# The sample's delta rule as two pairs of heads on 128 partitions instead of four heads on 64

## The chip, the cores and the metric

The kernel runs on one NeuronCore of a Trainium2 chip. The metric is device time in microseconds (us) of one execution. The engines named below are PE (TensorE matmul), DVE (VectorE), ACT (ScalarE), POOL (GpSimd) and SP (which issues most DMAs). PE works on fp32 data here in two ways: the large projections use fp32r operands split into a high and a low part, the small matrices of the delta rule use plain fp32, for which the trace shows two passes per product (and one pass per transpose).

## The reference, cut to what matters

One layer of a hybrid encoder is computed for two request groups that share weights: a prompt of 512 tokens and a sample of 64 tokens. The layer has a mixer (a gated delta rule with 4 heads of 128 x 128 state, and a differential attention with 4 heads), a cross attention to 256 memory tokens, and a feed-forward block of width 4096. The part that changes is the gated delta rule, in chunks of tokens:

```python
diff = G[..., :, None] - G[..., None, :]               # G: running sum of the gates
gam  = where(tril, exp(where(tril, diff, 0)), 0)
kk   = einsum('nbhid,nbhjd->nbhij', kc, kc)
a_sys = where(strict, bc[..., :, None] * kk * gam, 0) + eye(C)
u = triangular_solve(a_sys, bc[..., None] * vc)
w = triangular_solve(a_sys, (bc * exp(G))[..., None] * kc)
qk = einsum('nbhid,nbhjd->nbhij', qc, kc) * gam
...
vn = u - w @ S
o  = qg @ S + qk @ vn
S  = S * gl + kd.T @ vn                                # per head, chunk after chunk
```

The prompt starts from a zero state, the sample from `state_gdn`. The output `o` is normalised per head and token, and gated by silu(z).

## The kernel before, in words

All activations lie transposed, features on partitions and 576 tokens (512 prompt, then 64 sample) in the free dimension. The kernel runs through these stages: norm and transposes of x; twelve projections with a short convolution that give q, k and v of the delta rule (lines 401 to 419, kept in `cT`, a tile of [128, 4 heads, 576] for each); the gates (lines 430 to 496); the delta rule (lines 544 to 746); differential attention with its own projections (lines 776 to 893); memory keys and values, output projection, cross attention and the feed-forward block. A projection (`project`, line 165) is a run of matmuls into a bank tagged `pr`: 512 columns per pass with the high weights `wh`, 256 with the low weights `wl`, or 320 columns for the second part of the tokens.

The delta rule goes over five chunks (line 545): chunks 0 to 3 are 128 tokens of the prompt each, chunk 4 is the 64 tokens of the sample. For each chunk `gdn_prep` (line 566) does what doesn't need the state. For n tokens it transposes k, q and v of each head to tokens on partitions, makes the decay matrix `gam` (gates broadcast through a matmul with `triu`, exp on ACT, mask on POOL, line 603), KK times gam as `At`, KQ times gam, and then inverts the triangular matrix by doubling blocks (lines 632 to 680): at each level a masked part `B` of `At`, a product B,Dt that ACT copies to `Y`, a product with `X` that DVE subtracts from `Dt`, and transposes of `Dt` that ACT copies to `X`. With n = 64 that is one starting transpose and levels 2, 4, 8, 16, 32; with n = 128 level 64 comes on top. Every one of these steps loops over 4 heads, so that for chunk 4 each is four matmuls on 64 x 64 of the array.

`gdn_scan` (line 683) then goes through the state of a chunk: k times S, X times r, the output (q times S plus KQ times vn, two matmuls per head into one bank), kd times vn, the state's update on DVE, the norm, transposes, and the gate. Chunk 4 loads its own state S. At the top (lines 731 to 742) `gdn_prep` of chunk c + 1 is called ahead of `gdn_scan` of chunk c.

What stands where on each engine is decided when the program is built, by a scheduler that interleaves independent work, with program order as the priority: projections of z and of the differential attention are put between the steps of the delta rule. On its engine every instruction then runs in that order, and waits for its operands. PSUM banks are few: `pr` has three, `ba` two, and `g0`, `g1` (even and odd chunks) and `gs` (the scan) one each.

Of the kernel before, what the change touches and what calls it, by code (L numbers as in the profile page):

```python
# [8 lines left out]
F32 = mybir.dt.float32  # L9
F32R = mybir.dt.float32r  # L10
AF = mybir.ActivationFunctionType
# [23 lines left out]
def hybrid_layer_kernel(  # L35
# [107 lines left out]
    G.affine_select(out=triu, in_=triu, pattern=[[1, P]], compare_op=ALU.is_ge, fill=0.0, base=0, channel_multiplier=-1)  # L143

# [256 lines left out]
    for typ in (1, 0, 2):  # L401
        cT[typ] = (e5[:, 1], e2[:, 1], e2[:, 0])[typ]
        for h in range(H):
# [12 lines left out]
            A.activation(cT[typ][:, h, :SEQ], yv[:, :SEQ], AF.Silu)  # L416
            A.activation(cT[typ][:, h, SEQ:], yv[:, SOFF:n], AF.Silu)
# [18 lines left out]
    abT = small("p0", [16, T])  # L436
# [9 lines left out]
    for t, (t0, n) in enumerate(TT):  # L446
        tr(b[:n, t * 16 : t * 16 + 16], abT[:, t0 : t0 + n])
    ab2 = const([P, 5, 16], "ab2")
    V.memset(ab2[DEC:, 4, :], 0.0)
    V.tensor_copy(ab2[:, :4, :], b[:, :64].rearrange("p (t c) -> p t c", c=16))  # L450
    V.tensor_copy(ab2[:DEC, 4, :], b[:DEC, 64:80])
# [30 lines left out]
    V.tensor_scalar(gg, t3, -1.0, None, ALU.mult)  # L482
    V.memset(gg[DEC:, 4, :], 0.0)
# [12 lines left out]
    A.activation(kdc, kdc, AF.Exp)  # L496

# [46 lines left out]
    ck, cq, cv_ = cT[1], cT[0], cT[2]  # L544
    chunks = [(c, c * 128, c * 128, 128) for c in range(4)] + [(4, 512, 512, 64)]

    def v4(ap, n):
        return ap.rearrange("p (h n) -> p h n", h=4)[:, :, :n]
# [17 lines left out]
    def gdn_prep(c, c0, n):  # L566
        L = slice(c0, c0 + n)

        def st(tag):
            return sb(dict(gam="Y", sq="B", eg="B").get(tag, tag) + str(c % 2))  # L570

        r8 = tiny([P, 8], "tg")
        s8 = tiny([P, 8], "tg")
        bk = bank(f"g{c % 2}")
        for h in range(H):
            tr(bk[:n, h * P : (h + 1) * P], ck[:, h, L])
        kd = sb("kd")
        V.tensor_tensor(kd[:n], v4(bk, P)[:n], kdc[:n, c, :].unsqueeze(2).to_broadcast([n, 4, P]), ALU.mult)
        sq = st("sq")
        A.activation(sq[:n], v4(bk, P)[:n], AF.Square)  # L580
        V.tensor_reduce(s8[:n, 0:4], sq[:n], AX.X, ALU.add)
        bq = bank(f"g{c % 2}")
        for h in range(H):
            tr(bq[:n, h * P : (h + 1) * P], cq[:, h, L])
        sq2 = st("sq")
        A.activation(sq2[:n], v4(bq, P)[:n], AF.Square)
        V.tensor_reduce(s8[:n, 4:8], sq2[:n], AX.X, ALU.add)
        V.tensor_scalar(s8[:n], s8[:n], EPS, None, ALU.add)
        rpow(r8[:n], s8[:n])
        brk = tiny([P, 4], "tg")  # L590
        V.reciprocal(brk[:n], s8[:n, 0:4])
        V.tensor_tensor(brk[:n], brk[:n], beta[:n, c, :], ALU.mult)

        bg = bank(f"g{c % 2}")
        for h in range(H):
            mm(bg[:, h * P : h * P + n], bc(gg[:n, c, h : h + 1], [n, P]), triu[:n, :n])
        gam = st("gam")
        for h in range(H):
            V.tensor_scalar(
                gam[:n, h, :n], bg[:n, h * P : h * P + n], Gc[:n, c, h : h + 1], 0.0, ALU.subtract, ALU.min  # L600
            )
        A.activation(gam[:n, :, :n], gam[:n, :, :n], AF.Exp)
        G.tensor_tensor(gam[:n, :, :n], gam[:n, :, :n], triu[:n, :n].unsqueeze(1).to_broadcast([n, 4, n]), ALU.mult)
        bkk = bank(f"g{c % 2}")
        for h in range(H):
            mm(bkk[:n, h * P : h * P + n], ck[:, h, L], ck[:, h, L])
        At = st("At")
        for h in range(H):
            V.scalar_tensor_tensor(
                At[:n, h, :n], bkk[:n, h * P : h * P + n], brk[:n, h : h + 1], gam[:n, h, :n], ALU.mult, ALU.mult  # L610
            )
        bkq = bank(f"g{c % 2}")
        for h in range(H):
            mm(bkq[:n, h * P : h * P + n], ck[:, h, L], cq[:, h, L])
        KQ = sb("KQ")
        V.tensor_tensor(KQ[:n, :, :n], v4(bkq, n)[:n], gam[:n, :, :n], ALU.mult)
        nk, rq2 = tiny([P, 4], "tg"), tiny([P, 4], "tg")
        V.tensor_tensor(nk[:n], s8[:n, 0:4], r8[:n, 0:4], ALU.mult)
        V.tensor_scalar(r8[:n, 4:8], r8[:n, 4:8], P ** -0.5, None, ALU.mult)
        V.tensor_tensor(rq2[:n], r8[:n, 4:8], r8[:n, 4:8], ALU.mult)  # L620
        bv = bank(f"g{c % 2}")
        for h in range(H):
            tr(bv[:n, h * P : (h + 1) * P], cv_[:, h, L])
        vb = sb("vb")
        V.tensor_tensor(vb[:n], v4(bv, P)[:n], nk[:n].unsqueeze(2).to_broadcast([n, 4, P]), ALU.mult)
        if c > 0:
            eg = st("eg")
            A.activation(eg[:, :, :n], v4(bg, n), AF.Exp)
            G.tensor_tensor(ck[:, :, L], ck[:, :, L], eg[:, :, :n], ALU.mult)
            G.tensor_tensor(cq[:, :, L], cq[:, :, L], eg[:, :, :n], ALU.mult)  # L630

        def masked(lv):
            B = st("B")
            V.scalar_tensor_tensor(  # L634
                B[:n, :, :n], lev[:n, :n].unsqueeze(1).to_broadcast([n, 4, n]), float(lv), At[:n, :, :n],
                ALU.is_equal, ALU.mult,
            )
            return B

        X = sb("X")  # L640
        Dt = st("Dt")
        B = masked(1)
        V.tensor_tensor(X[:n, :, :n], ident[:n, :n].unsqueeze(1).to_broadcast([n, 4, n]), B[:n, :, :n], ALU.subtract)
        bt = bank(f"g{c % 2}")
        for h in range(H):
            tr(bt[:n, h * P : h * P + n], X[:n, h, :n])
        A.copy(Dt[:n, :, :n], v4(bt, n)[:n])
        lv = 2
        while lv < n:
            Y = st("Y")  # L650
            by = bank(f"g{c % 2}")
            if lv < 64:
                B = masked(lv)
                for h in range(H):
                    mm(by[:n, h * P : h * P + n], B[:n, h, :n], Dt[:n, h, :n])
                A.copy(Y[:n, :, :n], v4(by, n)[:n])
                bx = bank(f"g{c % 2}")
                if 2 * lv < n:
                    for h in range(H):
                        mm(bx[:n, h * P : h * P + n], X[:n, h, :n], Y[:n, h, :n])  # L660
                    V.tensor_tensor(Dt[:n, :, :n], Dt[:n, :, :n], v4(bx, n)[:n], ALU.subtract)  # L661
                    bt = bank(f"g{c % 2}")
                    for h in range(H):
                        tr(bt[:n, h * P : h * P + n], Dt[:n, h, :n])
                    A.copy(X[:n, :, :n], v4(bt, n)[:n])  # L665
                else:
                    for h in range(H):
                        mm(bx[:n, h * P : h * P + n], Y[:n, h, :n], X[:n, h, :n])
                    V.tensor_tensor(X[:n, :, :n], X[:n, :, :n], v4(bx, n)[:n], ALU.subtract)
            else:  # L670
                for h in range(H):
                    mm(by[64:, h * 64 : h * 64 + 64], At[:64, h, 64:], Dt[:64, h, :64])
# [8 lines left out]
        return dict(kd=kd, vb=vb, X=X, KQ=KQ, brk=brk, rq=r8[:, 4:8], rq2=rq2)  # L681

    def gdn_scan(c, c0, t0, n, q, S):
        L = slice(c0, c0 + n)
        if S is None:
            r = q["vb"]
        else:
            b = bank("gs")
            for h in range(H):
                mm(b[:n, h * P : (h + 1) * P], ck[:, h, L], S[:, h, :])  # L690
            r = sb("r", 1)
            V.tensor_tensor(r[:n], q["vb"][:n], v4(b, P)[:n], ALU.subtract)
        b = bank("gs")
        for h in range(H):
            mm(b[:n, h * P : (h + 1) * P], q["X"][:n, h, :n], r[:n, h, :])
        vn = sb("vn", 1)
        V.tensor_tensor(vn[:n], v4(b, P)[:n], q["brk"][:n].unsqueeze(2).to_broadcast([n, 4, P]), ALU.mult)
        bo = bank("gs")
        for h in range(H):
            o = bo[:n, h * P : (h + 1) * P]  # L700
            if S is not None:
                mm(o, cq[:, h, L], S[:, h, :], stop=False)
            mm(o, q["KQ"][:n, h, :n], vn[:n, h, :], start=S is None)
        b = bank("gs")
        for h in range(H):
            mm(b[:, h * P : (h + 1) * P], q["kd"][:n, h, :], vn[:n, h, :])
        Sn = S
        if S is None:
            Sn = sb("S")
            A.copy(Sn, v4(b, P))  # L710
# [487 lines left out]
```

## Time and profile before

| what | value |
|---|---|
| time, three runs | 1060.57, 1061.35 and 1063.02 us, median 1061.35 |
| the profiled execution's own time | 1062.43 us |
| its span, first to last instruction | 1060.4 us, granted PE clock 0.996 |
| busy: PE / PE weight loads / DVE / ACT / POOL | 1037.9 / 931.6 / 671.3 / 432.4 / 72.8 us |
| matmuls | 6574 |
| DMA | 89.96 MB, mean 85 GB/s |

The execution that was profiled took 2.0 us more than its span, and 1.1 us more than the median. In the rows below a line is: start in us, length in us, engine, source line, operation, written tile <- read tiles, shapes (for PE first the part of the array that is used, rows*columns, then the streamed operand), and xN where N neighbours were merged; in brackets stands idle time of the engine ahead of it and what ended it. Matmuls overlap in time, so the cost of one on PE is read from its start to the next one's start.

### The profile page before, as it was taken

What the parts mean: (1) busy time and instruction counts of PE and PEld (TensorE: products, weight loads), DVE (VectorE), ACT (ScalarE), POOL (GpSimd) and SP (SyncE); (2) the same over time, 40 slices, a digit from 0 to 9 for tenths busy, and PEclk for the clock granted to TensorE, in tenths of its full rate; (3) what the DMA queues carried; (4) which work ended last, traced back from release to release, by engine and by line L of the source; (5) the groups of instructions that cost most, each with busy time, mean ns of one, the idle gap of its engine ahead of it and who ended that gap; (6) DMA issues with size and microseconds to landing.
All of it is one profiled execution on the core that took longest, in us unless ns stands there. A gap on an engine that the chain in (4) does not pass through costs nothing.

```text
span 1060.4 us, 16925 instructions
## 1 busy us (share of the span) xinstructions
PE 1037.9 (98%) x6574; PEld 931.6 (88%) x6574; DVE 671.3 (63%) x1471; ACT 432.4 (41%) x897; POOL 72.8 (7%) x126
## 2 busy tenths in 40 slices
PE   8999999999999999999999999999999999999997
PEld 6999889898788877999887799999999999999986
DVE  6766684766466675564554666666666666666764
ACT  6644754333256665443333443323232323222344
POOL 4311120221000000000000000000000000000000
PEclk9999999999999999999999999999999999999999
DMA  7342310100132255634211222132414141323312
GB/s 212 109 126 70 122 40 21 43 1 22 41 100 64 69 187 193 176 87 139 58 42 40 59 81 63 58 100 60 117 49 123 42 119 50 110 60 110 90 50 90
DMA packets 139442, 89.96 MB, mean 85 GB/s; under 512 B 5522, under 2 KB 130576, under 8 KB 138852
## 3 DMA queue, kind: packets, MB, share of 16 engines
q1 hardware_dynamic: 138996, 88.24, 28.0%
q8 instruction: 52, 0.85, 0.3%
q10 hardware_dynamic: 368, 0.66, 0.2%
q14 instruction: 26, 0.21, 0.1%
HBM read 79.14 MB, written 9.74 MB: 84 GB/s over the span
## 4 chain that ended last, share of the span: by engine, by line
PE 88%; issue 4%; DVE 3%; ACT 2%; POOL 1%; DMA 1%; POOLq 0%; ACTq 0%; DVEq 0%
PE pr L103 68%; PE g L103 9%; PE gs L103 5%; PE ba L109 2%; PE g L109 2%; DMA raw<-in_w_ff_dram 1%; POOL tg L204 1%; PE ba L103 1%; DVE B L634 0%; ACT wh L157 0%; DVE wl L158 0%; POOL tiny L204 0%; PE pr L109 0%; DVE Dt L661 0%; PE gs L109 0%
## 5 line engine op out<-in xcount | busy, mean ns | idle before, releaser
L103 PE MATMUL pr<-u,wh 128*128 128x512 f32 (+1 forms) x2664 | 699.5, 344 | 1.2 <-DVE u L288 0.5
L103 PEld LDWEIGHTS pr<-u,wh 128*128 128x128 f32 x2664 | 457.7, 189 | 37.7 <-issue 1.5
L103 PE MATMUL pr<-u,wl 128*128 128x256 f32 (+1 forms) x1776 | 486.8, 300 | 0.0
L103 PEld LDWEIGHTS pr<-u,wl 128*128 128x128 f32 x1776 | 329.2, 189 | 8.3 <-issue 1.0
L157 ACT CAST wh<-raw 128x1024 fp32r<-128x1024 f32 (+1 forms) x153 | 136.5, 892 | 235.0 <-PE pr L103 223.2
L158 DVE TENSOR_TENSOR wl<-raw,wh 128x1024 fp32r<-128x1024 f32 (+1 forms) x153 | 157.4, 1029 | 60.4 <-ACT wh L157 58.5
L944 DVE TENSOR_TENSOR u<-u,pr 128x256 f32<-128x256 f32 (+1 forms) x160 | 72.4, 453 | 62.8 <-PE pr L103 60.2
L204 POOL TENSOR_TENSOR tiny<-tiny,nhalf 128x1 f32<-128x1 f32 (+4 forms) x11 | 10.1, 915 | 663.6 <-DVE tiny L1128 409.7
L197 ACT CAST u<-p 128x256 fp32r<-128x256 f32 x64 | 27.8, 434 | 51.8 <-DVE p L1065 51.8
L103 PE MATMUL pr<-wh,u 128*128 128x512 f32 x128 | 42.3, 404 | 0.0
L198 DVE TENSOR_TENSOR u<-p,u 128x256 fp32r<-128x256 f32 x64 | 29.3, 457 | 15.1 <-ACT u L197 15.1
L190 ACT COPY p<-pr 128x256 f32<-128x256 f32 (+1 forms) x44 | 16.4, 373 | 51.8 <-PE pr L103 51.8
L191 DVE TENSOR_TENSOR p<-pr,p 128x256 f32<-128x256 f32 (+1 forms) x44 | 18.6, 423 | 26.8 <-ACT p L190 26.8
L946 DVE TENSOR_TENSOR u<-u,pr 128x256 f32<-128x256 f32 x80 | 33.6, 420 | 2.4
L1064 DVE TENSOR_TENSOR p<-pr,rB 128x320 f32<-128x320 f32 x32 | 15.7, 492 | 25.7 <-PE pr L103 25.7
L415 DVE SCALAR_TENSOR_TENSOR p<-p,gcol,p 128x579 f32<-128x579 f32 x33 | 27.1, 821 | 6.4 <-ACT p L413 5.9
L1065 DVE SCALAR_TENSOR_TENSOR p<-p 128x256 f32<-128x256 f32 x64 | 29.3, 458 | 2.2
L665 ACT COPY X<-g 128x512 f32<-128x512 f32 (+1 forms) x24 | 13.2, 549 | 42.6 <-PE g L109 42.5
L200 ACT ACTIVATE u<-u,gcol 128x256 fp32r<-128x256 f32 (+1 forms) x32 | 17.0, 534 | 31.1 <-DVE u L946 31.1
L103 PE MATMUL g<-u,qz 128*128 128x256 f32 (+4 forms) x96 | 29.6, 412 | 0.0
L103 PEld LDWEIGHTS pr<-wh,u 128*128 128x128 f32 x128 | 23.6, 188 | 4.7 <-issue 0.2
L634 DVE SCALAR_TENSOR_TENSOR B<-lev,At 128x512 f32<-128x512 f32 (+1 forms) x30 | 20.8, 698 | 10.6 <-PE g L103 8.8
(315 smaller groups left out, 1214.3 us busy)
## 6 DMA issues: line engine op xcount, KB each, us to landing
raw<-in_w_ff_dram SPq DMA_DIRECT2D x32, 512.0 KB
raw<-in_w_ff_dram SPq DMA_DIRECT2D x64, 256.0 KB
raw<-in_w_in_dram SPq DMA_DIRECT2D x28, 512.0 KB
raw<-in_w_mem_k_dram SPq DMA_DIRECT2D x8, 512.0 KB
raw<-in_w_mem_v_dram SPq DMA_DIRECT2D x8, 512.0 KB
raw<-in_w_out_dram SPq DMA_DIRECT2D x8, 512.0 KB
raw<-in_w_mem_q_dram SPq DMA_DIRECT2D x8, 512.0 KB
raw<-in_w_mem_o_dram SPq DMA_DIRECT2D x8, 512.0 KB
```

The lines of the kernel that those rows point to most:

```text
L103: i = nc.tensor.matmul(out, lhsT, rhs, start=start, stop=stop)
L109: i = nc.tensor.transpose(out, in_, ident[:n, :n])
L157: A.copy(wh, raw)
L158: V.tensor_tensor(wl, raw, wh.bitcast(F32), ALU.subtract)
L197: A.copy(h, src)
L198: V.tensor_tensor(lo, src, h.bitcast(F32), ALU.subtract)
L204: G.tensor_tensor(out, in_, bc(nhalf[: in_.shape[0], 0:1], list(in_.shape)), ALU.pow)
L415: V.scalar_tensor_tensor(yv[:, :n], cb[:, i : i + n], cwt[:, m, i : i + 1], yv[:, :n], ALU.mult, ALU.add)
L634: V.scalar_tensor_tensor(B[:n, :, :n], lev[:n, :n].unsqueeze(1).to_broadcast([n, 4, n]), float(lv), At[:n, :, :n], ALU.is_equal, ALU.mult,)
L944: V.tensor_tensor(hm, hm, b, ALU.add)
L946: V.tensor_tensor(hm, hm, more, ALU.add)
L1065: V.scalar_tensor_tensor(f, f, 0.0, f, ALU.max, ALU.mult)
```

## The change

The sample's delta rule (chunk 4) is regrouped: two heads' tokens lie under each other on 128 partitions. What was four heads with 64 x 64 matrices becomes two pairs with 128 x 128 matrices that are block diagonal; the masks `triu2` and `ones2` (two blocks of 64) keep the heads of a pair apart, and the inversion stops at level 32 as before. In `cT` the sample's tokens are kept apart from the prompt's, so that two heads' 64 tokens are 128 neighbouring columns. The per-token columns (gates, their running sums, beta, decay) get copies in the pairs' layout, with a second running sum through `triu2` and `ones2`. In the scan of the sample the states of a pair stand beside each other as 256 columns, and `vn` is laid out as [128, pair, head, 128] with zeros where token and head don't belong together. The prompt's chunks keep their steps; they are written through the same helpers. The core of the diff:

```diff
+    ones2, triu2 = const([P, P], "ones2"), const([P, P], "triu2")
+    G.memset(ones2, 0.0)
+    for i in range(2):
+        R = slice(i * DEC, (i + 1) * DEC)
+        G.memset(ones2[R, R], 1.0)
+    G.tensor_tensor(triu2, triu, ones2, ALU.mult)
...
-        cT[typ] = (e5[:, 1], e2[:, 1], e2[:, 0])[typ]
+        flat = (e5[:, 1], e2[:, 1], e2[:, 0])[typ].rearrange("p k t -> p (k t)")
+
+        cT[typ] = [ap.rearrange("p (h t) -> p h t", h=H) for ap in (flat[:, : H * SEQ], flat[:, H * SEQ :])]
...
+    V.tensor_copy(abT[:, T:], abT[:, SEQ:T])
...
+    def halves_of(dst, src):
+
+        for i in range(2):
+            R = slice(i * DEC, (i + 1) * DEC)
+            V.tensor_copy(dst[R], src[R, 4, i::2])
+
+    halves_of(gg2, gg)
     V.memset(gg[DEC:, 4, :], 0.0)
...
+    halves_of(beta2, beta)
...
+    gsum2 = bank()
+    mm(gsum2[:, 0:2], triu2, gg2)
+    mm(gsum2[:, 2:4], ones2, gg2)
+    V.tensor_copy(Gc2, gsum2[:, 0:2])
+    V.tensor_tensor(kdc2, gsum2[:, 2:4], Gc2, ALU.subtract)
+    A.activation(kdc2, kdc2, AF.Exp)
...
+    chunks = [(c, 4, slice(c * P, (c + 1) * P)) for c in range(4)] + [(4, 2, slice(SEQ, T))]
...
+        def each(f, *args):
+
+            b = bank(f"g{c % 2}")
+            for i in range(nb):
+                f(b[:, i * P : (i + 1) * P], *(x(i) for x in args))
+            return v4(b, nb)
...
-        bkk = bank(f"g{c % 2}")
-        for h in range(H):
-            mm(bkk[:n, h * P : h * P + n], ck[:, h, L], ck[:, h, L])
+        bkk = each(mm, kb, kb)
...
+    def gdn_scan_sample(q, S):
...
+        b = pairs(each(lambda o, i: mm(o, kb(i), S2[:, i, :])))
...
+        def out(o, i):
+            mm(o, qb(i), S2[:, i, :], stop=False)
+            mm(o, q["KQ"][:, i, :], vw[:, i, :], start=False)
+
+        bo = pairs(each(out))
+        S = next_state(c, S, v4(each(lambda o, i: mm(o, q["kd"][:, i, :], vw[:, i, :])), 4))
+        on = sb("on", 1)[:, :nb]
+        normed(q, nb, [(R, bo[R, :, i, :]) for i, R in enumerate(own)], on)
...
+    A.copy(oa[:, 0, :, SEQ:], cT[0][1])
+    V.tensor_tensor(oa[:, 1, :, SEQ:], cT[0][1], oa[:, 0, :, SEQ:].bitcast(F32), ALU.subtract)
```

Since the scheduler sees other instructions, it also sets other orders. First, PE in the inversion of chunk 4, one level of it, before (`Dt` and `B` of this chunk, `pr` a projection, `on` and `gs` the scan of chunk 3):

```order
L109 MATMUL g_456_2561<-ident,Dt_439_2494 64x64 x4
L103 MATMUL pr_3122<-u_94,wh_3097 128x320
L103 MATMUL pr_3122<-u_94,wl_3098 128x320 x2
L103 MATMUL pr_3122<-u_94,wh_3097 128x320
L103 MATMUL g_458_2568<-Dt_439_2494,B_459_2569 64x64 x4
L109 MATMUL gs_2645<-ident,on_2637 128x128 x4
L103 MATMUL g_460_2576<-Y_457_2567,X_2493 64x64 x4
```

The same place now:

```order
L109 MATMUL g_457_2546<-ident,Dt_440_2497 128x128 x2
L103 MATMUL gs_2599<-vn_2588,kd_2202 128x128
L103 MATMUL pr_3091<-u_100,wl_3067 128x320
L103 MATMUL pr_3091<-u_100,wh_3066 128x320
L103 MATMUL g_460_2553<-Dt_440_2497,B_459_2551 128x128 x2
L103 MATMUL pr_3091<-u_100,wh_3066 128x320
L103 MATMUL pr_3124<-u_99,wh_3120 128x512
L103 MATMUL pr_3124<-u_99,wl_3121 128x256
L103 MATMUL g_461_2557<-Y_458_2550,X_2496 128x128 x2
```

Each group of four on 64 columns is now a group of two on 128 columns, and projections are spread otherwise between them.

Second, POOL at the start of the delta rule, before (`tg` is the power that gives 1/norm of a chunk, line 204; `Y` is `gam` of chunk 0, then of chunk 1, line 603):

```order
L204 TENSOR_TENSOR tg_1292<-tg_1293,nhalf 128x8
L204 TENSOR_TENSOR tg_1487<-tg_1488,nhalf 128x8
L603 TENSOR_TENSOR Y_176_1322<-Y_176_1322,triu 128x512
L603 TENSOR_TENSOR Y_226_1517<-Y_226_1517,triu 128x512
L204 TENSOR_TENSOR tiny_1203<-tiny_1201,nhalf 128x1
```

And now (the same lines have become 211 and 644):

```order
L211 TENSOR_TENSOR tg_1311<-tg_1312,nhalf 128x8
L644 TENSOR_TENSOR Y_177_1341<-Y_177_1341,triu 128x512
L211 TENSOR_TENSOR tg_1506<-tg_1507,nhalf 128x8
L644 TENSOR_TENSOR Y_227_1536<-Y_227_1536,triu 128x512
L211 TENSOR_TENSOR tiny_1222<-tiny_1220,nhalf 128x1
```

The mask of chunk 0 moved ahead of the power of chunk 1.

On ACT, a silu of z (line 562 before, 594 now) moved ahead of the table load and the exp that the chain of the gates needs (line 469 before, 477 now), and the exp of `kdc` (496, now 514) moved ahead of such a silu.

More of the change, by code (lines that the diff above doesn't have):

```diff
@@ L541, in hybrid_layer_kernel, with blocks, v4 @@
         V.tensor_tensor(lev, lev, triu, ALU.mult)
[L544 to L548, printed above, removed]
+    chunks = [(c, 4, slice(c * P, (c + 1) * P)) for c in range(4)] + [(4, 2, slice(SEQ, T))]
+    def blocks(typ, c, L):
+        if c < 4:
+            ap = cT[typ][0][:, :, L]
+        else:
+            ap = cT[typ][1].rearrange("p h t -> p (h t)").rearrange("p (b n) -> p b n", b=2)
+        return ap, lambda i: ap[:, i, :]
+    def v4(ap, nb):
+        return ap.rearrange("p (h n) -> p h n", h=4)[:, :nb, :]
     def sb(tag, bufs=2):
@@ L638, in masked @@
             return B
-        X = sb("X")
+        X = sb("X")[:, :nb]
         Dt = st("Dt")
         B = masked(1)
[L643 to L647, printed above, removed]
+        V.tensor_tensor(X, over(ident), B, ALU.subtract)
+        A.copy(Dt, each(tr, of(X)))
         lv = 2
-        while lv < n:
+        while lv < size:
@@ L680, in gdn_prep, with next_state, normed, gdn_scan @@
             lv *= 2
-        return dict(kd=kd, vb=vb, X=X, KQ=KQ, brk=brk, rq=r8[:, 4:8], rq2=rq2)
-    def gdn_scan(c, c0, t0, n, q, S):
-        L = slice(c0, c0 + n)
+        return dict(kd=kd, vb=vb, X=X, KQ=KQ, brk=brk, rq=rq, rq2=rq2)
+    def next_state(c, S, b):
+        if S is None:
+            S = sb("S")
+            A.copy(S, b)
+        else:
+            for h in range(H):
+                V.scalar_tensor_tensor(S[:, h, :], S[:, h, :], egl[:, c, h : h + 1], b[:, h, :], ALU.mult, ALU.add)
+        return S
+    def normed(q, nb, parts, out):
+        so, co = tiny([P, nb], "tg"), tiny([P, nb], "tg")
+        for R, src in parts:
+            A.activation(out[R], src, AF.Square)
+        V.tensor_reduce(so, out, AX.X, ALU.add)
+        V.tensor_tensor(so, so, q["rq2"], ALU.mult)
+        V.tensor_scalar(so, so, 1.0 / P, EPS, ALU.mult, ALU.add)
+        rpow(co, so)
+        V.tensor_tensor(co, co, q["rq"], ALU.mult)
+        for R, src in parts:
+            V.tensor_tensor(out[R], src, co[R].unsqueeze(2).to_broadcast(list(src.shape)), ALU.mult)
+    def gdn_scan(c, L, q, S):
+        (_, kb), (cq, qb) = (blocks(typ, c, L) for typ in (1, 0))
+        wide = [P, 4, P]
+        def each(f):
+            b = bank("gs")
+            for h in range(H):
+                f(b[:, h * P : (h + 1) * P], h)
+            return v4(b, 4)
         if S is None:
@@ L698, in gdn_scan @@
[L698 to L710, printed above, removed]
-        else:
-            for h in range(H):
-                V.scalar_tensor_tensor(
-                    Sn[:, h, :], S[:, h, :], egl[:, c, h : h + 1], b[:, h * P : (h + 1) * P], ALU.mult, ALU.add
-                )
@@ L725, in gdn_scan @@
-        bt = bank("gs")
-        for h in range(H):
-            tr(bt[:, h * P : h * P + n], on[:n, h, :])
-        V.scalar_tensor_tensor(cq[:, :, L], v4(bt, n), gn, zs[:, :, t0 : t0 + n], ALU.mult, ALU.mult)
-        return Sn
+            b = each(lambda o, h: mm(o, kb(h), S[:, h, :]))
+            r = sb("r", 1)
+            V.tensor_tensor(r, q["vb"], b, ALU.subtract)
+        b = each(lambda o, h: mm(o, q["X"][:, h, :], r[:, h, :]))
+        vn = sb("vn", 1)
+        V.tensor_tensor(vn, b, q["brk"].unsqueeze(2).to_broadcast(wide), ALU.mult)
@@ new lines, in out @@
+        def out(o, h):
+            if S is not None:
+                mm(o, qb(h), S[:, h, :], stop=False)
+            mm(o, q["KQ"][:, h, :], vn[:, h, :], start=S is None)
+        bo = each(out)
+        b = each(lambda o, h: mm(o, q["kd"][:, h, :], vn[:, h, :]))
+        S = next_state(c, S, b)
+        on = sb("on", 1)
+        normed(q, 4, [(slice(0, P), bo)], on)
+        bt = each(lambda o, h: tr(o, on[:, h, :]))
+        V.scalar_tensor_tensor(cq, bt, gn, zs[:, :, L], ALU.mult, ALU.mult)
```

201 lines of the change are left out of this document (96 added, 105 removed).

## The prediction

> **What bounds the kernel now.** I read the page first (busy time, then the chain that ended last), then PE's timeline in the stretch of the sample's chunk, then the timelines of PE, POOL and ACT where the delta rule begins. The page:
>
> ```profile
> PE 1037.9 (98%) x6574; PEld 931.6 (88%) x6574; DVE 671.3 (63%) x1471; ACT 432.4 (41%) x897; POOL 72.8 (7%) x126
> PE 88%; issue 4%; DVE 3%; ACT 2%; POOL 1%; DMA 1%; POOLq 0%; ACTq 0%; DVEq 0%
> ```
>
> PE is busy for 98% of the span and is 88% of the chain that ended last; while the delta rule goes through its steps, projections fill PE. So the change is worth what it takes off PE's own row, plus idle time of PE that comes or goes. What it does to DVE and ACT counts only where PE waits. Busy time hides cost, though, since matmuls overlap; I go by starts. Two groups of chunk 4 among projections (four transposes, then a product of four heads, two passes each):
>
> ```profile
> 274.13 0.41 PE L109 MATMUL g<-ident,Dt 64*64 64x64 f32 x4
> 274.47 0.39 PE L103 MATMUL pr<-u,wl 128*128 128x256 f32 x1
> 274.69 0.40 PE L103 MATMUL pr<-u,wh 128*128 128x512 f32 x1
> 274.93 0.28 PE L103 MATMUL pr<-u,wl 128*128 128x256 f32 x1
> 275.04 0.40 PE L103 MATMUL pr<-u,wh 128*128 128x512 f32 x1
> 275.37 0.67 PE L103 MATMUL g<-Dt,B 64*64 64x64 f32 x8
> 275.98 0.39 PE L103 MATMUL pr<-u,wl 128*128 128x256 f32 x1
> 276.20 0.40 PE L103 MATMUL pr<-u,wh 128*128 128x512 f32 x1
> 276.44 0.28 PE L103 MATMUL pr<-u,wl 128*128 128x256 f32 x1
> 276.55 0.39 PE L103 MATMUL pr<-u,wh 128*128 128x512 f32 x1
> ```
>
> An undisturbed 512 pass takes 276.44 - 276.20 = 0.24 us to the next start, a 256 pass 276.55 - 276.44 = 0.11. The 512 pass ahead of the product takes 0.33 (0.09 too much), the 256 pass behind it 0.22 (0.11 too much), the product itself 0.61. So one such group costs PE 0.81, and the transposes cost 0.34 + 0.11 behind + 0.09 ahead (taken alike) = 0.54. Now the same kinds of step on the full array, from chunks 1 and 2:
>
> ```profile
> 189.84 0.60 PE L109 MATMUL g<-ident,u 128*128 128x128 f32 x4
> 190.20 0.36 PE L103 MATMUL pr<-u,wl 128*128 128x256 f32 x1
> 190.40 0.39 PE L103 MATMUL pr<-u,wh 128*128 128x512 f32 x1
> ...
> 191.17 0.46 PE L103 MATMUL gs<-S,u 128*128 128x128 f32 x2
> ...
> 193.03 1.06 PE L103 MATMUL g<-u 128*128 128x128 f32 x8
> ```
>
> Four transposes and the 256 pass behind them take 0.56, that is 0.11 for each transpose and no edge. Sixteen passes of 128 columns take 193.03 - 191.17 = 1.86, 0.116 each, and nothing is lost between the two kinds in them (S, then KQ). So the full array pays by streamed columns alone, and the quarter array pays 0.2 us per group at its edges, and more inside.
>
> **Part by part: PE in chunk 4.** Columns streamed hardly change in the inversion (eight passes of 64 become four of 128); the edges go. Twelve products (two in each of five levels, KK and KQ): 0.81 becomes 4 x 0.116 = 0.46, 0.35 each, **-4.2**. Five groups of transposes (one at the start, four in the levels): 0.54 becomes 2 x 0.11 = 0.22, **-1.6**. The transposes of k, q and v: 12 become 6 at 0.11, **-0.7**. The gates' broadcast: eight passes become four, **-0.5** at 0.116. Then the scan, its first, second and third product before:
>
> ```profile
> 278.13 1.09 PE L103 MATMUL gs<-S,u 128*64 128x128 f32 x8
> ...
> 280.23 1.08 PE L103 MATMUL gs<-on,X 64*64 64x128 f32 x8
> ...
> 282.32 0.43 PE L103 MATMUL gs<-S,u 128*64 128x128 f32 x2
> ...
> 285.20 0.56 PE L103 MATMUL pr<-u,wh 128*128 128x320 f32 x2
> ```
>
> k times S is about 1.0 and two edges of 0.1, and becomes four passes of 256 columns, 0.93 at twice 0.116: -0.3. X times r, 1.2 with its edges, becomes four of 128: -0.7. The output took 285.20 - 282.32 = 2.88 for sixteen passes, 1.0 more than the sixteen above, since it alternates between two parts of the array; it becomes eight of 256, 1.86: -1.2 with its outer edges. kd times vn and the last transposes: -0.5. Scan **-2.7**. Together -9.7.
>
> Against that stands waiting. A group that finds its operand late shows it so, here on the full array:
>
> ```profile
> 155.02 0.36 PE L103 MATMUL pr<-u,wl 128*128 128x256 f32 x1
> 155.43 1.16 PE L103 MATMUL g<-Y,X 128*128 128x128 f32 x8
> 156.43 0.28 PE L103 MATMUL g<-Dt,B 128*128 128x128 f32 x1
> ```
>
> The 256 pass ahead lasts 0.41 instead of 0.11, the group 1.00 instead of 0.93: 0.37. The steps of chunk 4 are one chain, and the copies between them don't get shorter (ACT and DVE move 256 elements per partition as before), while PE's part does. I take five of some 27 groups to wait so, **+1.9**; bounds 0 and all 27, +10. I take a value near the low end because projections still stand between nearly all steps in the new order. The second running sum (`gsum2`) is four passes: **+0.5**. The extra DVE and POOL instructions (copies of columns, two masks, zeros in `vn`) lie on engines that PE doesn't wait for, except at the gates, next. If that cover failed, each would cost about its own length, 0.06 to 0.2 us.
>
> **Part by part: the start of the delta rule.** Here the order moved, and PE was idle:
>
> ```profile
> 107.91 1.28 ACT L469 ACT_TABLE_LOAD   x1
> 109.20 0.22 ACT L469 ACTIVATE t<-t 128x20 f32<-128x20 f32 x1
> 115.88 0.37 PE L103 MATMUL ba<-gg,triu 128*128 128x20 f32 x2 [0.60 <-DVE gg L483]
> 128.96 1.64 POOL L204 TENSOR_TENSOR tg<-tg,nhalf 128x8 f32<-128x8 f32 x1 [2.08 <-DVE tg L588]
> 130.57 1.28 POOL L603 TENSOR_TENSOR Y<-Y,triu 128x512 f32<-128x512 f32 x1
> 133.06 1.23 PE L103 MATMUL g<-u,u 128*128 128x128 f32 x8 [2.07 <-DVE At L609]
> 133.97 0.74 PE L103 MATMUL pr<-u,wh 128*128 128x512 f32 x1
> ...
> 137.08 0.56 PE L103 MATMUL g<-u 128*128 128x128 f32 x2
> ```
>
> At the gates a silu now stands ahead of the exp, so the exp starts about 1.0 us later (an add on DVE, then the silu, ahead of the same 1.28 us load), and with it the long DVE chain to `gg`; two small copies come on top, 0.3. PE has five more projection passes of 320 columns ahead of that product (0.15 each, from 0.24 for 512). So the idle 0.60 becomes about 0.6 + 1.3 - 0.7 = 1.2: **+0.6**.
>
> Then KQ of chunk 0 waits 2.07 us for `At`, which needs the mask on POOL; and that mask stood in POOL's queue behind the power of chunk 1, 128.96 to 130.57. In the new order it stands ahead of it. So it starts with its own operand (the exp on ACT, which by my count of the ACT rows ends at about the same time as before, near 128.1) instead of at 130.57: up to 2.4 earlier. PE also arrives about half a microsecond sooner. Idle 2.07 becomes 0.3: **-1.8**. And behind that idle time PE ran at half clock, by the windows:
>
> ```profile
> 134.00:137.00 3.00, 3.00 (x11) 2.60 (x11) 1.98 (x4) 2.97 (x4) 2.64 (x2) 0.50 0.25 58
> ```
>
> From 133.97 to 137.08 stand five 512 and four 256 passes, which take 1.64 at 0.24 and 0.11: 1.5 lost, **-1.5**. [...]
>
> Last, by the new order of PE the projections run up to 3.5 us ahead in the first three heads of the differential attention, which leaves less cover for its waits there: **+0.5**, bounds 0 and 3.5.
>
> **The sum**, against the profiled span: 1060.4 - 9.7 + 1.9 + 0.5 + 0.6 - 1.8 - 1.5 + 0.5 = 1050.9, 9.5 less. The profiled execution took 1062.43, the median is 1061.35; 9.5 off the median gives 1051.9.
>
> **The rivals.**
>
> A. The edges are waits for operands, not the price of changing the part of the array in use; then they stay. Of the -9.7, 0.2 us at each of some 22 edges is 4.4, and the time returns to 1056.3. For it: the groups' operands do come from ACT and DVE just ahead. Against it: the output of the scan pays 1.0 us for alternating although all its operands are there. Chance 0.10, 1055 to 1058.
>
> B. The start gains nothing, or loses: PE's wait for `At` stays, or the later `gg` leaves PE idle for 2 us, and half clock follows as at 134. Then -3.3 falls away and up to 1.5 comes: 1055.2 to 1056.7. [...] That rule alone has 0.02, B in all 0.17.
>
> C. Slower: the attention's heads run dry. The projections that move ahead are missing in heads 0 to 2, and PE waits in their softmax chains. It would take 0.5 us in each of the 20 tiles to eat the whole gain, 10 us, and more to give 1062 to 1066; it decides from 0.5 us per tile. Against it: in this stretch PE's row has no idle time before, and 3.5 us over the fifteen tiles of heads 0 to 2 is 0.2. Chance 0.05.
>
> ```profile
> 300.00:400.00 100.00, 99.99 (x588) 82.06 (x588) 68.34 (x224) 62.02 (x204) 4.17 (x6) 1.00 0.32 102
> ```
>
> D. More is gained: PE waits in chunk 4 no more than the projections cover (0 instead of 1.9), and idle time elsewhere in the prompt's chunks, whose order moved too, shrinks by a microsecond or two. 1047 to 1049.5. Chance 0.10.
>
> **How the numbers follow.** The forecast (0.58) has 1049.5 to 1055 as its own range. The range over the cases, 1047.5 to 1058, leaves out C, and the edges of A and D. A measurement of this kernel can tell 0.2%, 2.1 us, so faster means under 1059.2: nearly all of the forecast, A, B and D, 0.90; within 0.2% takes A's and B's upper tail, 0.05; slower is C, 0.05.
>
> **What would show it.** In the profile after: PE's rows of chunk 4 in the form 128*128 x4 with 256 passes behind them at 0.2 or less, and the output of the scan at about 1.9 us; PE's product of `gg` at an idle of 1 to 1.5 and KQ of chunk 0 at under 0.8, with 1.00 as granted clock behind it; the start of the state's update of chunk 4 (PE, kd times vn) still with idle time near 0.8 to 1.0, since the norm's chain through POOL stays. I am wrong if PE's passes around chunk 4 keep edges of 0.1, if new idle times above 1 us stand in PE's waits between 140 and 420 us, or if the granted clock shows a second stretch of 0.50.

## The result and the profile after

The changed kernel took 1054.21 us (median of four runs, 1053.19 to 1054.83), the kernel before 1060.96 beside it (1060.31 to 1063.02). The ratio is 0.9936, 95% interval 0.9924 to 0.9947: 6.75 us less, where 9.5 were forecast. The profiled execution took 1053.76 with a span of 1052.0.

Busy time and the chain that ended last, on the page after:

```profile
PE 1027.7 (98%) x6488; PEld 925.7 (88%) x6488; DVE 673.8 (64%) x1478; ACT 433.7 (41%) x900; POOL 73.1 (7%) x130
PE 88%; DVE 5%; issue 3%; ACT 2%; POOL 1%; DMA 1%; POOLq 0%; ACTq 0%; SPq 0%; DVEq 0%
```

PE is still busy for 98%, with 86 passes fewer; the share of DVE in the chain grew from 3 to 5%. PE's timeline in chunk 4, one of the new groups that waits for its operand and one that hardly does, and the weight load of the first, which names the wait:

```profile
262.19 0.45 PE L103 MATMUL pr<-u,wh 128*128 128x320 f32 x2
262.58 0.71 PE L103 MATMUL g<-Dt,B 128*128 128x128 f32 x4
263.05 0.39 PE L103 MATMUL pr<-u,wl 128*128 128x320 f32 x1
...
270.09 0.68 PE L103 MATMUL g<-Dt,B 128*128 128x128 f32 x4
270.53 0.36 PE L103 MATMUL pr<-u,wl 128*128 128x256 f32 x1
270.73 0.39 PE L103 MATMUL pr<-u,wh 128*128 128x512 f32 x1
```

```profile
262.58 0.52 PEld L103 LDWEIGHTS g<-Dt,B 128*128 128x128 f32 x4 [0.20 <-ACT X L685]
```

The product at 270.09 costs 0.44 and 0.08 at the pass behind it (0.20 instead of 0.117): 0.52. The one at 262.58 costs 0.47, 0.08 behind it, and 0.10 ahead, where two passes of 320 take 0.39 instead of 0.29 until it starts: 0.65. Counted so, the twelve products of chunk 4 take 6.8 us, 0.57 each, against 0.81 for the group before that the prediction showed and the forecast's 0.46. In all ten products of the levels the first weight load starts 0.05 us after the copy on ACT that releases it; in the kernel before, one of the ten came so close.

PE's timeline at the start of the delta rule, the waits in it (dots between):

```profile
116.41 0.37 PE L103 MATMUL ba<-gg,triu 128*128 128x20 f32 x2 [0.72 <-DVE gg L500]
...
130.74 1.16 PE L103 MATMUL g<-u,u 128*128 128x128 f32 x8 [0.26 <-DVE At L648]
131.65 0.36 PE L103 MATMUL pr<-u,wl 128*128 128x256 f32 x1
131.86 0.40 PE L103 MATMUL pr<-u,wh 128*128 128x512 f32 x1
132.10 0.28 PE L103 MATMUL pr<-u,wl 128*128 128x256 f32 x1
...
137.77 1.10 PE L109 MATMUL ba<-ident,u 128*128 128x128 f32 x8 [0.81 <-DVE tiny L234]
...
151.50 0.33 PE L109 MATMUL g<-ident,Dt 128*128 128x128 f32 x1 [1.03 <-DVE Dt L684]
```

The idle time of 2.07 ahead of KQ is 0.26, and a 512 pass behind it takes 0.24 where such passes took 0.43 before, with 1.00 as granted clock from 131 to 137 us, so the half clock is gone. But two idle times are new: 0.81 for the transposes of the memory tokens, 1.03 for a `Dt` of chunk 0.

Where the time went, by stretches of PE's row. From the length of each stretch I take what its passes cost undisturbed (0.235 us for 512 columns of a projection, 0.147 for 320, 0.117 for 256, 0.87 ns per column for all others, from the 0.112 at which passes of 128 columns follow each other); waits, edges and low clock are left. "Before" is a second profiled execution of the kernel before (span 1058.6; its run stands with the experiments), since in the first the passes ran slowly for longer at the start. Chunk 4 starts on PE just ahead of the sixth row, which also holds the last part of chunk 3.

```
stretch of PE                           before   after   change
start to 30 us                            8.06    8.06     0.0
30 us to the product of gg                2.28    2.95    +0.7
gg to KQ of chunk 0                       3.10    1.89    -1.2
KQ of chunk 0 to idle at vb (200 us)      8.26    9.48    +1.2
to kd times vn of chunk 2                 4.34    4.46    +0.1
to the last transposes of chunk 4        11.43    5.57    -5.9
to the norm of attention head 0           6.69    5.81    -0.9
the rest                                 13.54   13.51     0.0
passes themselves, undisturbed          990.55  989.44    -1.1
```

That is 7.1 less up to the last matmul, and 6.6 in the spans. The row of chunk 4 gave 5.9, and chunk 4 most of the 1.1, about as much as the whole. The start of the delta rule (rows two to four), forecast at -2.7, lost 0.7; 0.45 of that is the second running sum `gsum2`, which stands there and was forecast apart at +0.5.

### The profile page after: what moved, and what is told of

Same layout as the page of the kernel before. It is cut to its first block, busy times and chain, and to the rows that moved or that the text cites. A ratio compares the mean times of both kernels' runs of the same rounds, so it can differ in the third digit from the quotient of the medians.

```text
span 1052.0 us, 16768 instructions
## 1 busy us (share of the span) xinstructions
PE 1027.7 (98%) x6488; PEld 925.7 (88%) x6488; DVE 673.8 (64%) x1478; ACT 433.7 (41%) x900; POOL 73.1 (7%) x130
## 4 chain that ended last, share of the span: by engine, by line
PE 88%; DVE 5%; issue 3%; ACT 2%; POOL 1%; DMA 1%; POOLq 0%; ACTq 0%; SPq 0%; DVEq 0%
PE pr L103 69%; PE g L103 9%; PE gs L103 5%; PE ba L109 2%; PE g L109 2%; DMA u<-in_cache_mem_k_dram 1%; DVE wl L165 1%; POOL tg L211 1%; PE ba L103 0%; DMA S<-in_state_gdn_dram 0%; POOL tiny L211 0%; DVE B L668 0%; DVE X L674 0%; DVE Dt L684 0%; PE pr L109 0%
## 5 line engine op out<-in xcount | busy, mean ns | idle before, releaser
L164 ACT CAST wh<-raw 128x1024 fp32r<-128x1024 f32 (+1 forms) x153 | 136.4, 892 | 233.7 <-PE pr L103 220.1
```

What stands on the lines that cost most here:

```text
L164: A.copy(wh, raw)
```

## The experiments

The times stand against the kernel before on the same chip, 1060.3 to 1060.7 us.

**a1: only the order on POOL.** The kernel before, with one dependency more, without a semaphore:

```diff
         rpow(r8[:n], s8[:n])
+        if c == 1:
+            tc.add_manual_dep(
+                nc.cur_bb.bb.instructions[-1], mask0[0],
+                mybir.DependencyInfo(mybir.DependencyClass.NoSync, mybir.DependencyReason.DATA),
+                reason="mask first",
+            )
...
+        if c == 0:
+            mask0.append(nc.cur_bb.bb.instructions[-1].name)
```

> The kernel before, with one order changed: on POOL the mask of chunk 0 stands ahead of the power of chunk 1, as in the changed kernel. Chunk 4 stays in four heads. By the prediction's step for the start of the delta rule (idle ahead of KQ 2.07 to 0.3, half clock behind it gone) it is 3.3 us faster than before, near 1057.7 us. Rival, read from the trace of the changed kernel (two new idle times of 0.81 and 1.03 us at 137.8 and 151.5): the chain of chunk 0 runs on DVE and ACT, PE only reaches its next wait sooner, and 0 to 1 us is left, 1060 to 1061; then the idle of 2.07 is gone in the profile and new ones of 1 to 2 us in all stand between 135 and 155 us.

Measured: 1059.07 us, ratio 0.9985 (0.9977 to 0.9994), 1.6 less. Its PE at the same place:

```profile
129.99 0.49 PE L103 MATMUL g<-u 128*128 128x128 f32 x2 [0.45 <-ACT B L638]
130.31 1.06 PE L103 MATMUL g<-u,u 128*128 128x128 f32 x8
...
134.06 0.66 PE L109 MATMUL g<-ident,u 128*128 128x128 f32 x4 [0.40 <-DVE KQ L626]
```

The 2.07 became 0.45 and 0.40, and no idle time of 1 us follows by 155 us. So neither the step of the prediction nor its rival has it: the move is worth half of the 3.3. By the table's count a1 gains 1.5 up to KQ, and only 0.5 from there to 200 us, where the half clock's 1.5 should have come back. And the two new idle times of the changed kernel don't come with this move alone: they belong to the rest of its new order.

**b1: the sample's scan by heads again.** The changed kernel, with k times S, X times r and the output in 64 wide pieces; shown is the output:

```diff
-        def out(o, i):
-            mm(o, qb(i), S2[:, i, :], stop=False)
-            mm(o, q["KQ"][:, i, :], vw[:, i, :], start=False)
+        def out(o, i, j, R):
+            mm(o, qb(i)[:, R], S2[:, i, j * P : (j + 1) * P], stop=False)
+            mm(o, q["KQ"][R, i, R], vw[R, i, j * P : (j + 1) * P], start=False)
```

> The changed kernel, with k times S, X times r and the output of the sample's scan done head by head again, 64 columns or rows of the array at a time, in the layout of the pairs. By the prediction's terms for these three (0.3, 0.7 and 1.2) it takes 2.2 us more than the changed kernel, about 1056.4; its output alternates between two parts of the array and takes 2.9 us instead of 1.8. Rival (the edges are waits for operands): the same time as the changed kernel within 0.5 us, and the output near 1.9.

Measured: 1056.46 us, ratio 0.9957 (0.9942 to 0.9972), 2.25 more than the changed kernel's 1054.21. The output in the changed kernel, and then in b1:

```profile
279.35 0.67 PE L103 MATMUL gs<-S,u 128*128 128x256 f32 x2
279.85 0.59 PE L103 MATMUL gs<-vn,KQ 128*128 128x256 f32 x2
...
281.15 0.60 PE L109 MATMUL ba<-ident,p 128*128 128x128 f32 x4
```

```profile
281.08 0.43 PE L103 MATMUL gs<-S,u 128*64 128x128 f32 x2
281.44 0.43 PE L103 MATMUL gs<-vn,KQ 64*64 64x128 f32 x2
...
283.97 0.66 PE L109 MATMUL ba<-ident,p 128*128 128x128 f32 x4
```

1.80 against 2.89, with nothing idle in either: 0.36 for two passes of 128 columns (281.08 to 281.44), where two of the full array take 0.22 to 0.23. So the output's part of the scan's term is shown by its mechanism too, and the three parts together by their time, within what the two intervals allow.

**c1 and c2: the price of one edge.** An edge is what a change to a part of the array or back costs. The kernel before with 56 products (two passes each) among the projections of the feed-forward stage, shown for c1; c2 loads all 128 rows and columns of `ident` as weights and still streams 64 columns:

```diff
+    def probe():
+        mm(db[:64, :64], ident[:64, :64], ident[:64, :64], pin=True)
```

> The kernel before, with 56 products more in the feed-forward stage, each of 64 x 64 on a quarter of the array (two passes of 64 columns, operands constant, nobody reads the result), put between two projection passes where PE never waits. If changing the part of the array in use has a price of 0.2 us for a pair of edges, each costs 0.116 + 0.2 = 0.32 us, 18 us in all: about 1079. If the edges are waits for operands, each costs 0.116, 6.5 us in all: about 1067.5.

> The kernel before, with 56 products more at the same places, now 64 columns on the full array of 128 x 128 (two passes, operands constant). Both theories: 0.116 us each, 6.5 us in all, about 1067.5. If it costs as much as the quarter, it is the fp32 product between fp32r passes that costs, not the part of the array.

Measured: c1 1086.87 us, 26.2 more, 0.47 each; c2 1072.49, 11.8 more, 0.21 each. One of them in c1, then one in c2:

```profile
752.49 0.40 PE L103 MATMUL pr<-u,wh 128*128 128x512 f32 x1
752.73 0.28 PE L103 MATMUL pr<-u,wl 128*128 128x256 f32 x1
752.94 0.32 PE L103 MATMUL g<-ident 64*64 64x64 f32 x2
753.20 0.50 PE L103 MATMUL pr<-u,wh 128*128 128x512 f32 x1
753.53 0.40 PE L103 MATMUL pr<-u,wl 128*128 128x256 f32 x2
```

```profile
748.15 0.40 PE L103 MATMUL pr<-u,wh 128*128 128x512 f32 x1
748.39 0.28 PE L103 MATMUL pr<-u,wl 128*128 128x256 f32 x1
748.51 0.33 PE L103 MATMUL g<-ident 128*128 128x64 f32 x2
748.65 0.48 PE L103 MATMUL pr<-u,wh 128*128 128x512 f32 x1
748.97 0.40 PE L103 MATMUL pr<-u,wl 128*128 128x256 f32 x2
```

From the start of the first 512 pass to that of the last 256 pass shown is 1.04 us in c1 and 0.82 in c2, where the three projection passes alone take 0.235 + 0.117 + 0.235 = 0.59. So c1's product costs 0.45 and c2's 0.23. No operand is late here, so the price is the array's: two passes of 64 columns cost 0.12 on a quarter (0.058 each inside the groups of before), and the change to a quarter and back 0.34. That is the difference of 0.35 that the prediction used for a product, and more than the 0.2 of this expectation, which had left out what the group loses inside (0.61 for eight passes that take 0.47 at 0.058). The weight loads show where it goes, first in c1, then in c2:

```profile
752.94 0.19 PEld L103 LDWEIGHTS g<-ident 64*64 64x64 f32 x2 [0.26 <-issue]
```

```profile
748.40 0.31 PEld L103 LDWEIGHTS g<-ident 128*128 128x128 f32 x2
```

In c2 the load starts together with the pass ahead (748.39); in c1 it starts 0.21 after that pass (752.73), and the profile names nothing that it waits for. What holds it for that time isn't shown. And c2 is no cheaper than 0.21: both theories had half of that. A pass of 64 columns on the full array costs as much as one of 128: 0.23 for the two in c2, where two passes of 128 columns take 0.22 to 0.23.

**e1: full array, but passes of 64 columns.** The changed kernel, with each product of chunk 4's preparation in two halves (the loop of such a product):

```diff
+            for i in range(nb):
+                for R in (slice(0, DEC), slice(DEC, P)):
+                    mm(b[:, i * P + R.start : i * P + R.stop], x(i), y(i)[:, R])
```

> The changed kernel, with the twelve products and the gates' broadcast of the sample's preparation done in halves: eight passes of 64 columns on the full array instead of four of 128, the same columns in all, as many passes as the kernel before had on a quarter of the array. If the preparation gained because the part of the array in use no longer changes, this costs nothing: within 0.7 us of the changed kernel, 1053.5 to 1054.8 us. Rival: it gained because there are half as many passes; then 2 to 4 us come back, 1056 to 1058.

Measured: 1059.04 us, ratio 0.9982 (0.9973 to 0.9992), 4.9 more than the changed kernel's 1054.1. One such product among others:

```profile
266.71 1.10 PE L103 MATMUL g<-Dt,B 128*128 128x64 f32 x8
267.65 1.12 PE L103 MATMUL gs<-vn,kd 128*128 128x128 f32 x8
268.52 0.48 PE L103 MATMUL pr<-u,wh 128*128 128x512 f32 x1
```

Eight passes of 64 columns take 0.94 (266.71 to 267.65), with 0.05 for a late operand in it, as much as eight of 128 behind them. Thirteen such groups at 0.45 more are 5.8; 4.9 came, by the table's count all of it in the row of chunk 4 (10.48 instead of 5.57). So the full array alone would have given little: with eight passes of 64 columns a product costs 0.9 there, no less than on a quarter with its edges (0.81). The gain takes both, no change of the part in use and 128 columns per pass, and two heads together bring both. Every pass loads its own weights in this kernel (on the pages 6574 loads for 6574 matmuls before, 6488 for 6488 after), and with 64 columns streamed the passes of a product follow each other at 0.112 where the weights have 128 columns (here with 128 rows, in the gates' broadcast of the kernel before with 64) and at 0.058 where they have 64 (in the inversion before with 64 rows, in KQ before with 128). So in these traces the spacing goes by the columns of the weights, not by their rows; what sets it isn't shown.

**d1, d2, d4, d5: the two new idle times and the start.** The changed kernel with, in turn: (d1) the two products of k and q by the decay on DVE, not POOL (`G.tensor_tensor(ck, ck, eg, ...)` becomes `V.`, `cq` too); (d2) the loop of the memory tokens' norm written behind `gdn_prep` of chunk 0; (d4) the masks `ones2` and `triu2` made behind the first steps; (d5) all three.

> The changed kernel, with the two products of k and q by the decay (lines 663 and 664) on DVE instead of POOL. In the trace of the changed kernel PE is idle for 1.03 us at 151.5 for a subtraction on DVE (line 684) that stands behind a weight subtraction of 2.29 us, during which POOL ran the second of these products. If POOL's work beside it is what stretches DVE, the weight subtraction returns to some 1.2, the idle shrinks by 0.5 or more, and the time is 0.5 to 1.5 us less than that of the changed kernel, 1052.7 to 1053.7. Rival: DVE's own order sets it, the two products add 1.2 us to DVE in each chunk, and the time is the same or 1 to 2 us more.

> The changed kernel, with the norm and the transposes of the memory tokens written behind the preparation of chunk 0 instead of ahead of it, so that PE finds the start of the inversion of chunk 0 ahead of these transposes. If the idle of 0.81 us at 137.8 and the wait of chunk 0 behind it are what the new order lost, they go, and the time is 0.8 to 1.5 us less than that of the changed kernel, 1052.7 to 1053.4. Rival: the chain of chunk 0 is the bound there and the idle moves by some us, 0 to 0.3 less.

> The changed kernel, with the masks of the pairs (ones2, triu2) made at some 20 us instead of at the start. In the trace of the changed kernel the first product waits for POOL at 2.37 instead of for a DMA at 2.25, and the first scaling on DVE takes 1.47 instead of 1.30 beside POOL's triu2. If these two shift all that follows, 0.3 us less than the changed kernel, under what a time can tell, but seen in the profile: the first projection pass starts 0.3 earlier than at 14.26. Rival: the idle ahead of the first projection takes it up.

> The changed kernel with all three: decay products on DVE, memory tokens behind chunk 0, masks late. If the three losses are separate, 1.5 to 3 us less than the changed kernel, 1051.2 to 1052.7. Rival: they are one and the same chain, and it gives no more than the best of the three alone.

Measured, as ratios beside 0.9936: d1 0.9924 (0.9908 to 0.9941), 1052.81 us; d2 0.9972 (0.9960 to 0.9984), 1057.50; d4 0.9929 (0.9914 to 0.9944), 1053.08; d5 0.9935 (0.9920 to 0.9950), 1053.76. By time only d2 differs clearly from the changed kernel (0.9924 to 0.9947), and it is slower; for the others the traces decide. What d1 removes stands on DVE and POOL of the changed kernel:

```profile
146.67 1.36 DVE L674 TENSOR_TENSOR X<-ident,B 128x512 f32<-128x512 f32 x1
147.95 2.29 DVE L165 TENSOR_TENSOR wl<-raw,wh 128x1024 fp32r<-128x1024 f32 x1
150.16 0.68 DVE L668 SCALAR_TENSOR_TENSOR B<-lev,At 128x512 f32<-128x512 f32 x1
150.76 0.68 DVE L684 TENSOR_TENSOR Dt<-Dt,g 128x512 f32<-128x512 f32 x1
```

```profile
146.20 1.28 POOL L663 TENSOR_TENSOR u<-u,B 128x512 f32<-128x512 f32 x1 [5.20 <-PE pr L103]
147.43 1.73 POOL L664 TENSOR_TENSOR u<-u,B 128x512 f32<-128x512 f32 x1
```

The weight subtraction takes 2.29 while POOL works until 149.16, and the subtraction for which PE waits stands behind it. In d1 there is no such POOL work:

```profile
148.72 1.22 DVE L165 TENSOR_TENSOR wl<-raw,wh 128x1024 fp32r<-128x1024 f32 x1
149.87 0.68 DVE L668 SCALAR_TENSOR_TENSOR B<-lev,At 128x512 f32<-128x512 f32 x1
150.88 0.69 DVE L684 TENSOR_TENSOR Dt<-Dt,g 128x512 f32<-128x512 f32 x1 [0.33 <-PE g L103]
```

It takes 1.22, now DVE waits for PE, and PE's idle time of 1.03 is gone (its `Dt` transposes start at 151.62 without one). In the changed kernel 1.21 of the 2.29 lie ahead of POOL's end and 1.08 behind it. How POOL's work holds DVE up isn't shown, only that the 2.29 are 1.22 without it.

d1 also takes away an idle time that isn't new: 1.45 at 200.9, which the kernel before has too (1.47). In the changed kernel DVE waits there for the second of POOL's products, and PE for what DVE does behind it (`vb`, v scaled per token):

```profile
199.55 0.69 DVE L668 SCALAR_TENSOR_TENSOR B<-lev,At 128x512 f32<-128x512 f32 x1 [1.18 <-POOL u L664]
...
200.90 0.66 PE L109 MATMUL g<-ident,X 128*128 128x128 f32 x4 [1.45 <-DVE vb L659]
```

In d4 the first projection pass starts at 13.97 instead of 14.26, as expected, too little to tell by time. d2 went the other way: 3.3 us more than the changed kernel, where 0.8 to 1.5 less was expected. In its trace the idle time of 0.81 is gone, but that of 1.03 is 1.22 (at 149.85), and the memory tokens' scalings stand on DVE where they stood (136.9 and 138.9, in the changed kernel 136.4 and 138.5). The loss comes later: by the table's count 1.8 between 200 us and kd times vn of chunk 2, with a new idle time of 0.60 at 201.5 and another of 0.51 at 215.8, and 2.0 in the attention's stretch. What brings it there isn't shown. d5, which holds d2's edit, ends where the changed kernel does.

**Two of them, and both kernels once more.** d6 is the changed kernel with the edits of d1 and d4.

> The changed kernel with two of the three edits: decay products on DVE and masks of the pairs late. If the gains of the two alone (ratios 0.9924 and 0.9929 against 0.9936) are real and add up, its ratio to the kernel before is near 0.992, 1052.0 us; the idle of 1.03 us at 151 is not there and the first projection pass starts near 14.0. Rival: both were noise, and it stands where the changed kernel stands, 0.9936.

> The changed kernel itself, once more, so that it can be compared on one chip with the version of two edits, and to see when its PE reaches full clock. In eight profiles so far full clock came at 12.5 to 14.7 us or at 18.5 to 19.0, whichever kernel it was (before: 18.5, changed: 13.1). Expected: ratio 0.9936 as before, and full clock at one of these two times. If full clock came early because of the change, it comes near 13 again in every profile of it.

> The kernel before, once more, for its profile. Full clock came at 18.5 us in its profiled execution. If the time of full clock differs from execution to execution, it comes at 12.5 to 14.7 or at 18.5 to 19 here, and in the first case the span is 1.5 to 2 us shorter than 1060.4 with nothing else changed. If the late clock belongs to this kernel, it comes at 18.5 again.

Measured: d6 1051.82 us, ratio 0.9921 (0.9907 to 0.9934), runs 1051.64 to 1053.45; the changed kernel beside it 1054.10, 0.9939 (0.9927 to 0.9952), runs 1053.36 to 1054.93. d6 is the best version; the intervals overlap a little. By the table's count it gains 2.7 between KQ of chunk 0 and 200 us (9.48 to 6.81), mostly the new idle time of 1.03 and the old one of 1.45, and gives 2.0 back in the attention's stretch (5.80 to 7.82). The kernel before once more: 1060.39, 0.9994 (0.9983 to 1.0004), span 1058.6 instead of 1060.4. Its first seven projection passes of 512 columns, first in the profile that the prediction used, then in the second:

```profile
13.97 3.35 PE L103 MATMUL pr<-u,wh 128*128 128x512 f32 x7 [0.55 <-DVE u L288]
```

```profile
13.96 1.88 PE L103 MATMUL pr<-u,wh 128*128 128x512 f32 x7 [0.61 <-DVE u L288]
```

3.35 us against 1.88: most of these passes take 0.43 from start to start in the first and 0.235 in the second. 0.43 is also what a 512 pass took at 134 us of the kernel before, where the granted clock is 0.50. So I call the faster passes full clock, though the column of the granted clock has 1.00 for the whole start. The changed kernel's two profiles had full clock at 13.1 and 12.2, but b1 and d1, with the same start, at 19.0 and 18.7. So this differs from execution to execution, and 1.4 us of the 8.7 between the first two profiled executions (1062.43 and 1053.76) are not the change's.

## Why the prediction was right, and where it was not

**PE in chunk 4: right.** -9.7 with +1.9 of waiting, -7.8 in all; the trace gives -5.9 of waits and edges and -1.1 of passes, -7.0. The products' part was mis-sized: -4.2 was forecast, 12 x (0.81 - 0.57) = -2.9 measured, and the difference of 1.3 is waiting for operands, which the +1.9 was for. Waiting came as some 0.1 at most groups, not as five at 0.37: all ten products of the levels now start at ACT's copy, so the copies, and not PE, set when they start. The scan was -2.7; undoing its three larger parts, priced at 2.2, cost 2.25.

One sentence of this part was wrong without harm: "the full array pays by streamed columns alone". Under 128 columns it doesn't (0.23 us for two passes of 64 in c2, 0.112 for one in e1). All passes of the pairs have 128 or 256, so the sum didn't meet it.

**One wait unforeseen.** k times S of the sample now waits for the load of its state:

```profile
274.36 0.31 PE L103 MATMUL pr<-u,wl 128*128 128x320 f32 x1
274.99 0.45 PE L103 MATMUL gs<-S,u 128*128 128x256 f32 x1 [0.32 <-DMA S<-in_state_gdn_dram]
```

```profile
269.93 0.37 SPq L160 DMA_DIRECT2D raw<-in_w_in_dram  x1
270.35 0.57 SPq L811 DMA_DIRECT2D S<-in_state_gdn_dram  x1
```

0.32 here, 0.76 in the second profile of the changed kernel. In SP's queue a load of projection weights now stands just ahead of the state's load; in the kernel before none stands between it and the store of the prompt's state. No run issued the load earlier. The prediction asked nowhere whether a transfer would be in time for a PE that comes earlier. The wait of the state's update, left at 0.8 to 1.0, fell to 0.41.

**The start: the step that failed.** "Idle 2.07 becomes 0.3: -1.8" and "-1.5" for the half clock came about at their place (0.26, and 0.24 for a 512 pass). That the half clock comes with the idle time of 2.07 also held: the four profiled executions that have it (2.06 to 2.07, both of the kernel before, c1 and c2) have 0.50 behind it for 3.4 us; the ten others have neither. But both were booked as gains to the end, without asking what is late next, and by the table gg to 200 us ends where it began (-1.2 and +1.2). PE came earlier to KQ and, without the half clock, to what stands behind it, and then waited for the memory tokens (0.81) and for a `Dt` behind a stretched weight subtraction (1.03), which the new order had put ahead. a1 shows that the POOL move by itself is worth 1.6, d1's trace that the second idle time was the POOL work's doing. Which of the other moved instructions took the rest isn't settled; d2 was one attempt, and failed. The cause of that rest stays open. The idle at `gg` grew by 0.1, not 0.6, though its stretch lost 0.7. The prediction had named "new idle times above 1 us" between 140 and 420 us as the sign of its being wrong; one came, and it is this step.

**The attention: wrong in sign.** +0.5 was forecast, -0.9 measured. No run tested why.

**The rivals.** A, edges as waits, fell: c1 has them at 0.34 with constant operands, and b1 brought them back; what true waits there are is the 1.3 above. B, a start that gains nothing, came true for the start in its size and not in its mechanism, while the whole time stayed 1.0 under its 1055.2: neither the wait for `At` nor a long idle at `gg` did it. A further delay from the moved silu, to which B gave 0.02, is shown by no run: in the profile after, the exp starts 1.29 behind the start of its table load of 1.28 (108.04 and 109.33), as it did before, and the idle at `gg` is 0.72. C and D didn't happen. The median came 2.3 us over the forecast and within its own range: the start, without `gsum2`, fell short by 2.9 and chunk 4 by 0.8, and the attention gave 1.4 more. The last was luck: with the +0.5 that was forecast for it the median would have been 1055.6, above the forecast's own 1049.5 to 1055.

## What to carry to other kernels

Small matrices next to big ones paid here for the change to a part of the array and back, 0.34 us each time (c1); on the full array each pass of their products took as long with 64 columns streamed as with 128, 0.112 us (e1). What avoided the two was putting them together as blocks, until weights and streamed columns are both 128 wide: 0.57 us a product, with what it waits, against 0.81.

A stall that went was worth here only what the next late operand left, 1.6 us of 3.3 (a1): follow the chain on the other engines from that place on before booking it.

Before comparing two profiles, look whether their first stretch ran at the same clock: here 1.4 of the 8.7 us between the first two came from it.

## What the hardware showed that was not expected

- A pass of 64 columns of a product on the full array costs 0.112 us, as one of 128 (e1); on a quarter of the array 0.058 (the inversion of the kernel before).
- The change to a quarter of the array and back costs 0.34 us with all operands there (c1).
- At the start, PE's passes ran at the slower spacing (0.43 us for 512 columns instead of 0.235) until 12.2 to 14.7 us in some profiled executions and until 18.5 to 19.0 in others, of the same kernel too, worth some 1.4 us.
- A DVE instruction on 8 columns took 0.94 us beside POOL's mask from 127.82 to 129.11 (0.16 in the kernel before, where it ended just ahead of POOL's start):

```profile
127.82 1.30 POOL L644 TENSOR_TENSOR Y<-Y,triu 128x512 f32<-128x512 f32 x1 [1.72 <-ACT Y L643]
128.20 0.94 DVE L633 TENSOR_SCALAR tg<-tg 128x8 f32<-128x8 f32 x1
```
